# A one-layer hybrid decoder on one core: differential-attention weights split into two float32r halves, conv halos copied from PSUM, and one joint values product

## The chip, the core and the metric

The kernel runs on one core of one Trainium2 chip. The metric is the device time of one execution in microseconds (us); lower is better. Several executions were timed, and one more was recorded by the hardware profiler. The core has a matrix engine (TensorE, PE in the profile, with weight loads shown apart as PEld), three elementwise engines (VectorE = DVE, ScalarE = ACT, GpSimd = POOL), and a queue (SyncE = SP) that issues the DMAs here.

## The reference, cut to what the change touches

One layer maps 2048 tokens of width 1024 through three token mixers (a gated delta net, GDN; a dilated window attention; a differential attention), an output product, a LayerNorm, and a gated feed-forward block (FFN) with a short causal convolution. In the differential attention each of four heads has two softmax maps over the same values, and the second is subtracted with a weight:

```python
s = jnp.einsum('bhmqd,bhmkd->bhmqk', q_blk, k).astype(f32) * scale
s = jnp.where(kpos[None, :] <= qpos[:, None], s, -jnp.inf)
p = jax.nn.softmax(s, axis=-1)
return jnp.einsum('bhqk,bhkd->bhqd', p[:, :, 0] - lam * p[:, :, 1], v)
```

Both the GDN input and the FFN pass through a depthwise causal convolution over tokens:

```python
for j in range(1, K):
    y = y + xp[:, j:j + T] * w[j]
```

with K = 4 for the GDN and K = 3 for the FFN. The values of the dilated and of the differential attention are 256 columns each of one input product `x @ w_in`.

## The kernel before, in words

Tokens are cut into four blocks of 512 (`TB`). A product in full precision is made of three float32r products: each operand is split into a high half `hi` (a float32r cast) and a low half `lo` (the rest), and hi·hi, hi·lo and lo·hi are added in PSUM (lines 172 to 179). `weights` (lines 118 to 132) prepares the halves of a weight tile: one 512 KB DMA to `wraw`, a cast on ScalarE to `whi` (L130), a subtraction on GpSimd to `wlo` (L131). Such a tile serves 24 matmuls of 512 columns in a plain product.

Jobs are named by a letter and a token block: `A` projects for both attentions (`Projection.project`), `G` projects for the GDN with its convolution (`GatedInput.project`), `d` is the differential attention (`Diff.block`), `w` the dilated one, `i`, `b`, `p`, `r` are the stages of the GDN (invert, merge, prepare, recur), `o`, `t` and `f` are the output product, a transposition and the FFN block. Three lists, `FIRST`, `SECOND` and `THIRD` (lines 1331 to 1333), give the order in which the program is written; a scheduler of the framework then sets the order of the instructions on every engine by its own estimate of the times, and so mixes jobs. The GDN jobs are in `SECOND`, and the second list's PSUM pools are opened where the first list's are closed. Each engine carries out its own instructions in order.

**Values.** `Projection.values` (line 609) runs twice a block: once for the dilated attention (kind 0), whose stationary operand takes every fourth token, `v[k][:, n::4]`, and once for the differential one (kind 1), with 128 tokens side by side. The moving operand is 256 columns wide; a kind takes 96 matmuls and 2 weight tiles for a block.

**Weighted.** `Diff.weighted` (line 774) makes, for each pair of heads `i`, block `b` and 128 keys `kt`, and for each head `hh` of the pair, one step: two score matmuls (L796), two exponentials on ScalarE to `pd` and `pe` (L798), `pd = pd + nlam * pe` on VectorE (L802), and in the diagonal block a causal mask on GpSimd (L806). Two steps later (`LAG_PD`) a plain float32 matmul (L781) multiplies `pd` with 64 columns of values into half of the bank `po`. There are 160 steps: 16 in `d0`, 32, 48 and 64 in `d1` to `d3`.

**Halo.** A convolution copies a finished product from PSUM to `ub` behind the last 2 or 3 columns of the block before, kept in `halo` (GDN lines 328 to 330, 48 times; FFN lines 1052 to 1054, 172 times). Then one multiplication (L332, L1056) and two or three multiply-adds (L335, L1058) run on VectorE.

## Time and profile before

| what | value |
|---|---|
| median of 3 runs | 3292.51 us (3289.01 to 3293.84) |
| the profiled execution | 3297.27 us, its span 3295.6 us |
| mean granted TensorE clock | 0.967 |
| ScalarE busy | 1466.8 us (45%) |
| GpSimd busy | 1163.7 us (35%) |
| DMA moved | 434.19 MB, mean 132 GB/s |

The span runs from the first to the last instruction of the profiled execution. Busy times of TensorE add up instructions that overlap in its pipeline, so the cost of one matmul is read from the distance between two starts, not from its duration.

### The profile page before, as it was taken

To read this page: it belongs to the slowest core of one execution; us is meant where nothing else is said; L and a number is where in the kernel's file an instruction comes from. 1 tells how busy PE (TensorE), PEld (TensorE's weight loads), DVE (VectorE), ACT (ScalarE), POOL (GpSimd) and SP (SyncE) were. 2 spreads that over 40 slices of the span, in tenths; PEclk is the share of its full clock that TensorE was granted. 3 is DMA by queue.
4 is the path that set the end of the run, shared out by engine and by line. 5 is a ranking of instruction groups with operands and counts; after the bars stand their busy time and mean duration, and the time that the engine had idled before them with its cause. 6 is when DMAs were issued, how large, how long until landed. Compare 5 with 4: busy or idle time off the path is not lost. (4 is left out here: it accounts for less than half of the span.)

```text
span 3295.6 us, 42011 instructions
## 1 busy us (share of the span) xinstructions
PE 3073.1 (93%) x14860; PEld 2381.1 (72%) x14860; DVE 2328.9 (71%) x3958; ACT 1466.8 (45%) x2790; POOL 1163.7 (35%) x617
## 2 busy tenths in 40 slices
PE   7999987898898999999989999999999999999998
PEld 6768876676786787767866677777777664777776
DVE  3572689869557458777898667768988654787667
ACT  3543352343435335544755443344566445333223
POOL 3452443333225223334333332223333331344443
PEclk8999988998999999999999999999999998999999
DMA  6436373453756734333534334363533332432322
GB/s 201 147 132 191 105 215 110 132 155 104 216 169 185 232 108 138 104 97 115 169 99 147 98 106 133 99 201 102 181 104 108 96 93 74 132 121 90 96 85 82
DMA packets 286994, 434.19 MB, mean 132 GB/s; under 512 B 54624, under 2 KB 174944, under 8 KB 286016
## 3 DMA queue, kind: packets, MB, share of 16 engines
q1 hardware_dynamic: 286784, 431.51, 42.6%
q8 instruction: 117, 1.92, 0.2%
q14 instruction: 93, 0.76, 0.1%
HBM read 365.03 MB, written 66.26 MB: 131 GB/s over the span
## 5 line engine op out<-in xcount | busy, mean ns | idle before, releaser
L131 POOL TENSOR_TENSOR wlo<-wraw,whi 128x1024 fp32r<-128x1024 f32 x412 | 1011.2, 2456 | 1753.2 <-ACT whi L130 1577.1
L176 PE MATMUL d<-xhi,whi 128*128 128x512 f32 x2144 | 859.4, 401 | 27.1 <-ACT xhi L137 7.9
L178 PE MATMUL d<-xhi,wlo 128*128 128x512 f32 x2144 | 860.6, 402 | 15.3 <-POOL wlo L131 15.2
L177 PE MATMUL d<-xlo,whi 128*128 128x512 f32 x2144 | 856.6, 400 | 5.5 <-DVE xlo L139 5.5
L130 ACT CAST whi<-wraw 128x1024 fp32r<-128x1024 f32 x412 | 430.0, 1045 | 435.0 <-issue 160.0
L176 PEld LDWEIGHTS d<-xhi,whi 128*128 128x128 f32 x2144 | 411.4, 192 | 129.2 <-ACT whi L130 14.8
L178 PEld LDWEIGHTS d<-xhi,wlo 128*128 128x128 f32 x2144 | 411.1, 192 | 128.3 <-POOL wlo L131 23.0
L177 PEld LDWEIGHTS d<-xlo,whi 128*128 128x128 f32 x2144 | 411.2, 192 | 104.5 <-issue 13.8
L1054 DVE COPY c_halo<-ub 128x2 f32<-128x2 f32 x172 | 208.8, 1214 | 120.2 <-ACT ub L1053 119.6
L1121 PE MATMUL rp<-whi,hhi 128*128 128x512 f32 x704 | 268.8, 407 | 21.1 <-DVE r L1131 7.6
L1122 PE MATMUL rp<-wlo,hhi 128*128 128x512 f32 x704 | 282.2, 403 | 3.1 <-POOL wlo L131 2.9
L1124 PE MATMUL rp<-whi,hlo 128*128 128x512 f32 x672 | 269.8, 403 | 0.4 <-DVE hlo L1083 0.4
L739 ACT ACTIVATE bank<-bank,nm 128x512 f32<-128x512 f32 (+3 forms) x320 | 191.0, 597 | 130.5 <-DVE nm L735 72.9
L802 DVE SCALAR_TENSOR_TENSOR pd<-pe,f_nlam,pd 128x512 f32<-128x512 f32 (+3 forms) x160 | 138.0, 870 | 94.6 <-ACT pe L798 83.9
L735 DVE TENSOR_REDUCE nm<-bank 128x1 f32<-128x512 f32 (+3 forms) x288 | 163.3, 593 | 46.4 <-PE bank L730 45.9
L1121 PEld LDWEIGHTS rp<-whi,hhi 128*128 128x128 f32 x704 | 135.2, 193 | 61.5 <-issue 17.1
L1075 ACT ACTIVATE yg<-yg 128x512 f32<-128x512 f32 x88 | 55.5, 631 | 261.9 <-DVE yv L1074 250.7
L1058 DVE SCALAR_TENSOR_TENSOR yg<-ub,c_taps,yg 128x512 f32<-128x512 f32 x176 | 169.6, 963 | 2.4
L1122 PEld LDWEIGHTS rp<-wlo,hhi 128*128 128x128 f32 x704 | 135.6, 193 | 40.3 <-issue 6.8
L1124 PEld LDWEIGHTS rp<-whi,hlo 128*128 128x128 f32 x672 | 129.3, 193 | 34.6 <-issue 6.3
L1131 DVE TENSOR_TENSOR r<-r,rp 128x512 f32<-128x512 f32 x152 | 100.6, 681 | 69.6 <-PE rp L1124 61.2
L781 PE MATMUL bank<-pd,fv 128*64 128x512 f32 (+3 forms) x320 | 145.2, 563 | 4.3 <-DVE pd L802 2.2
(280 smaller groups left out, 5023.7 us busy)
## 6 DMA issues: line engine op xcount, KB each, us to landing
wraw<-in_w_up SPq DMA_DIRECT2D x172, 512.0 KB
wraw<-in_w_down SPq DMA_DIRECT2D x84, 512.0 KB
wraw<-in_w_gdn SPq DMA_DIRECT2D x64, 512.0 KB
ks<-fk_d SPq DMA_DIRECT2D x160, 196.0 KB
wraw<-in_w_out SPq DMA_DIRECT2D x40, 512.0 KB
wraw<-in_w_att SPq DMA_DIRECT2D x32, 512.0 KB
yraw<-y_d SPq DMA_DIRECT2D x48, 256.0 KB
xraw<-in_xT SPq DMA_DIRECT2D x40, 256.0 KB
```

The costliest lines, as they stand in the source:

```text
L130: nc.scalar.copy(hi, raw)
L131: nc.gpsimd.tensor_tensor(out=lo, in0=raw, in1=hi, op=ALU.subtract)
L176: nc.tensor.matmul(out=ps, lhsT=whi[:, k], rhs=xhi[k], start=(k == 0), stop=False)
L177: nc.tensor.matmul(out=ps, lhsT=whi[:, k], rhs=xlo[k], start=False, stop=False)
L178: nc.tensor.matmul(out=ps, lhsT=wlo[:, k], rhs=xhi[k], start=False, stop=(k == KD - 1))
L735: nc.vector.tensor_reduce(out=o, in_=s[:, 0:nf], axis=mybir.AxisListType.X, op=ALU.min)
L739: nc.scalar.activation(out=s[:, 0:n], in_=s[:, 0:n], func=AF.Exp, scale=-1.0, bias=o, accum_out=den[:, b, m, qt : qt + 1])
L1054: nc.vector.tensor_copy(self.halo[:, mt], ub[:, TB : TB + 2])
L1058: nc.vector.scalar_tensor_tensor(out=yc, in0=ub[:, j : j + TB], scalar=self.taps[:, mt, j : j + 1], in1=yc, op0=ALU.mult, op1=ALU.add)
L1121: nc.tensor.matmul(out=ps, lhsT=hi[:, sl], rhs=whi, start=first, stop=False)
L1122: nc.tensor.matmul(out=ps, lhsT=hi[:, sl], rhs=wlo, start=False, stop=last and lo is None)
L1124: nc.tensor.matmul(out=ps, lhsT=lo[:, sl], rhs=whi, start=False, stop=last)
```

## The change

Four things are changed.

1. The differential weights: `pe` now takes the sum, then ScalarE casts it to float32r (`ph`) and GpSimd subtracts that to get the rest (`pl`). The values are stored as 128 columns for each head, 64 high and 64 low, side by side. Two float32r matmuls (`ph`, then `pl`) past these 128 columns give the two halves of the result in the two halves of `po`'s partitions, and they are added at the end, once per head. One head is done after the other: `weighted` is called per head, `po` belongs to one head at a time. The product is three steps behind (`LAG_PD = 3`), `pd` has 2 buffers instead of 6, as `pe` has.
2. Each load of keys takes 2 maps of 256 keys instead of 4 of 128, and each load of values 2 x 128 columns; the number of loads is the same.
3. The convolutions: ScalarE copies the halo into `ub`, and VectorE saves the next halo from PSUM instead of from `ub`.
4. The values of both attentions are one product with 512 moving columns: 96 matmuls of 512 columns for a block instead of 192 of 256 (384 instead of 768 in all), 8 weight loads instead of 4 for a block, each serving 12 matmuls; the stationary operand is 128 tokens side by side for both. Two PSUM tiles are filled at a time.

```diff
-                nc.vector.tensor_copy(ub[:, 0:3], self.halo[:, mt])
+                nc.scalar.copy(ub[:, 0:3], self.halo[:, mt])
                 nc.scalar.copy(ub[:, 3:], pp)
-                nc.vector.tensor_copy(self.halo[:, mt], ub[:, TB : TB + 3])
+                nc.vector.tensor_copy(self.halo[:, mt], pp[:, TB - 3 : TB])
...
-        ws = [dn.weights(self.I["w_val"][kind, j], k=4, m=256) for j in range(2)]
         for g in range(2):
...
+            ps = [dn.ps.tile([P, TB], F32, tag="d", name="vp") for _ in range(2)]
+            for j in range(KD // 2):
+                whi, wlo = dn.weights(self.I["w_val"][j], k=2, m=TB)
+                for a in range(2):
+                    k = 2 * j + a
+                    for i in range(2):
+                        sl = slice((2 * g + i) * P, (2 * g + i + 1) * P)
+                        xhi, xlo = (v[k][:, sl] for v in x)
+                        nc.tensor.matmul(out=ps[i], lhsT=xhi, rhs=whi[:, a], start=(k == 0), stop=False)
+                        nc.tensor.matmul(out=ps[i], lhsT=xhi, rhs=wlo[:, a], start=False, stop=False)
+                        nc.tensor.matmul(out=ps[i], lhsT=xlo, rhs=whi[:, a], start=False, stop=(k == KD - 1))
+            for i in range(2):
...
+                nc.scalar.copy(vo, ps[i][:, 0:256])
+                nc.sync.dma_start(out=wide[n * P : (n + 1) * P].rearrange("t i c -> t (i c)"), in_=vo)
...
+                nc.scalar.copy(vs[:, :, 0], src)
+                nc.vector.tensor_tensor(out=vs[:, :, 1], in0=src, in1=vs[:, :, 0], op=ALU.subtract)
...
-            for hh in range(2):
-                nc.tensor.matmul(out=po[64 * hh : 64 * hh + 64, q0:], lhsT=v[:, 64 * hh : 64 * hh + 64],
-                                 rhs=pd[hh][:, q0:], start=start, stop=stop)
+            for part in (0, 1):
+                nc.tensor.matmul(out=po[:, q0:], lhsT=v, rhs=parts[part][:, q0:], start=start and part == 0, stop=stop and part == 1)
...
-                    pd = bp.tile([P, TB], F32, tag="pd", name="pd", bufs=NPD)
+                    pd = bp.tile([P, TB], F32, tag="pd", name="pd", bufs=NPE)
...
-                    nc.vector.scalar_tensor_tensor(out=pd[:, q0:], in0=pe[:, q0:], scalar=self.nlam, in1=pd[:, q0:],
+                    nc.vector.scalar_tensor_tensor(out=pe[:, q0:], in0=pe[:, q0:], scalar=self.nlam, in1=pd[:, q0:],
...
+                    ph = bp.tile([P, TB], F32R, tag="ph", name="ph", bufs=LAG_PD + 1)
+                    nc.scalar.copy(ph[:, q0:], pe[:, q0:])
+                    pl = bp.tile([P, TB], F32R, tag="pl", name="pl", bufs=LAG_PD + 1)
+                    nc.gpsimd.tensor_tensor(out=pl[:, q0:], in0=pe[:, q0:], in1=ph[:, q0:], op=ALU.subtract)
...
-            nc.vector.tensor_copy(ob, po)
+            o = ob[64 * hh : 64 * hh + 64]
+            nc.scalar.copy(o, po[64:P])
+            nc.vector.tensor_tensor(out=o, in0=po[0:64], in1=o, op=ALU.add)
...
-NPD = 6
...
-LAG_PD = 2
+LAG_PD = 3
```

The order of the instructions moves with it. On TensorE, where the GDN begins (`kk`, L420, is its first matmul), there stands before, in the middle of the convolution products `d` of job G1:

```order
L178 MATMUL d<-xhi,wlo 128x512
L420 MATMUL kk<-k 128x128
L176 MATMUL d<-xhi,whi 128x512
L177 MATMUL d<-xlo,whi 128x512
L420 MATMUL kk<-k 128x128 x3
```

and in the changed kernel, inside the values product `vp` of block 1:

```order
L624 MATMUL vp<-whi,xlo 128x512
L622 MATMUL vp<-whi,xhi 128x512 x2
L420 MATMUL kk<-k 128x128 x4
L623 MATMUL vp<-wlo,xhi 128x512
L624 MATMUL vp<-whi,xlo 128x512
```

Ahead of that first `kk` stood 1056 matmuls of products `d` and 384 of values; now 768 and 170 stand there, and 16 instead of 32 of the small product L304. From the first `kk` to the last GDN matmul (L565) stand 1344 `d` instead of 1056, 118 values instead of 192, and the same 182 of the output product; behind it 4320 `d` as before, 96 values instead of 192, and all the `weighted` products but those of `d0`.

On GpSimd, in the stage where `d2` runs among the FFN's products, only the mask stood between the halves of the weights before:

```order
L131 TENSOR_TENSOR wlo<-wraw,whi 128x1024 x9
L806 AFFINE_SELECT pd<-pd 128x128
L131 TENSOR_TENSOR wlo<-wraw,whi 128x1024
L806 AFFINE_SELECT pd<-pd 128x128 x3
L131 TENSOR_TENSOR wlo<-wraw,whi 128x1024
```

and now, at the start of `d2`, one or two subtractions `pl` stand ahead of each `wlo`:

```order
L819 TENSOR_TENSOR pl<-pe,ph 128x512
L131 TENSOR_TENSOR wlo<-wraw,whi 128x1024 x3
L819 TENSOR_TENSOR pl<-pe,ph 128x512 x2
L131 TENSOR_TENSOR wlo<-wraw,whi 128x1024
L819 TENSOR_TENSOR pl<-pe,ph 128x512 x2
```

On VectorE, in the FFN of the last block (`yg` and `yv` are the two convolutions, `hlo` the low half of the hidden tile), two small copies stood around each convolution before:

```order
L1052 COPY ub<-c_halo 128x2
L1054 COPY c_halo<-ub 128x2
L1056 TENSOR_SCALAR yv<-ub,c_taps 128x512
L1058 SCALAR_TENSOR_TENSOR yv<-ub,c_taps,yv 128x512 x2
L1074 TENSOR_TENSOR yv<-yv,yg 128x512
```

and now one, which reads the PSUM tile `d`:

```order
L1067 COPY c_halo<-d 128x2
L1069 TENSOR_SCALAR yv<-ub,c_taps 128x512
L1071 SCALAR_TENSOR_TENSOR yv<-ub,c_taps,yv 128x512 x2
L1087 TENSOR_TENSOR yv<-yv,yg 128x512
L1089 SCALAR_TENSOR_TENSOR yv<-yg,yv 128x512
```

The other small copy went to ScalarE's queue; the multiplication follows the remaining one as it did.

More of the change, by code (lines that the diff above doesn't have):

```diff
@@ L607, in product, with values @@
         return (yield from self.dn.product(w or self.dn.weights(self.I["w_att"][mt]), x))
-    def values(self, kind, x, dst):
+    def values(self, x, wide, near):
         nc, dn = self.nc, self.dn
-        ws = [dn.weights(self.I["w_val"][kind, j], k=4, m=256) for j in range(2)]
         for g in range(2):
-            ps = dn.ps.tile([P, 2, 256], F32, tag="d", name="vp")
-            for j in range(2):
-                n = 2 * g + j
-                for k in range(KD):
-                    whi, wlo = (w[:, k % 4] for w in ws[k // 4])
-                    xhi, xlo = (v[k][:, n::4] if kind == 0 else v[k][:, n * P : (n + 1) * P] for v in x)
-                    nc.tensor.matmul(out=ps[:, j], lhsT=xhi, rhs=whi, start=(k == 0), stop=False)
-                    nc.tensor.matmul(out=ps[:, j], lhsT=xhi, rhs=wlo, start=False, stop=False)
-                    nc.tensor.matmul(out=ps[:, j], lhsT=xlo, rhs=whi, start=False, stop=(k == KD - 1))
-                    yield SLOT
-            vo = self.ap.tile([P, 2, 2, 2, P], F32, tag="y", name="vo", bufs=NY)[:, 0]
-            nc.scalar.copy(vo, ps.rearrange("p j (i c) -> p i j c", i=2))
-            nc.sync.dma_start(out=dst[:, :, 2 * g : 2 * g + 2], in_=vo)
@@ new lines, in values @@
+            for i in range(2):
+                n = 2 * g + i
+                vo = self.ap.tile([P, 2, TB], F32, tag="y", name="vo", bufs=NY)[:, 0, 0:256]
+                nc.scalar.copy(vo, ps[i][:, 0:256])
+                nc.sync.dma_start(out=wide[n * P : (n + 1) * P].rearrange("t i c -> t (i c)"), in_=vo)
+                vs = self.ap.tile([P, 2, 4, 2, 64], F32R, tag="y", name="vs", bufs=NY)[:, 0]
+                src = ps[i][:, 256:].rearrange("p (h c) -> p h c", h=4)
+                nc.scalar.copy(vs[:, :, 0], src)
+                nc.vector.tensor_tensor(out=vs[:, :, 1], in0=src, in1=vs[:, :, 0], op=ALU.subtract)
+                nc.sync.dma_start(out=cast(near[:, :, n]), in_=cast(vs.rearrange("p h x c -> p h (x c)")))
@@ L662, in project @@
                     nc.sync.dma_start(out=cast(dst[32 * g : 32 * g + 32, mm]).rearrange("p m t -> m p t"), in_=parts[g])
-        for kind, dst in ((0, wv_d), (1, v_d)):
-            yield from self.values(kind, x, dst)
-        blocks[t] = (q_d, k_d, v_d, wq_d, wk_d, wl_d, wv_d)
+        yield from self.values(x, wv_d, v_d)
+        blocks[t] = (q_d, k_d, v_d, wq_d, wk_d, wl_d, wv_d.rearrange("(j r) i c -> j i r c", r=4))
 class Diff:
@@ L772, in stats, with weighted @@
         self.later.append([LAG_TURN, turn])
-    def weighted(self, t, i, qs):
+    def weighted(self, t, i, hh, qs, ob):
         nc, bp = self.nc, self.bp
@@ L795, in weighted @@
                         s = self.ps_s.get(False)
-                        nc.tensor.matmul(out=s[:, q0:], lhsT=ks[:, 2 * hh + m],
-                                         rhs=qs[:, 2 * hh + m, q0:], start=True, stop=True)
+                        nc.tensor.matmul(out=s[:, q0:], lhsT=ks[:, m, j * P : (j + 1) * P], rhs=qs[:, 2 * hh + m, q0:], start=True, stop=True)
                         nc.scalar.activation(out=e[:, q0:], in_=s[:, q0:], func=AF.Exp, scale=-1.0)
@@ L844, in block @@
             for i in range(2):
-                yield from self.weighted(t, i, qs[i])
+                ob = self.bp.tile([P, TB], F32, tag="ob", name="ob", bufs=1)
+                for hh in range(2):
+                    yield from self.weighted(t, i, hh, qs[i], ob)
             while self.later:
@@ L1051, in conv @@
         ub = hp.tile([P, TB + 2], F32, tag="ub", name="ub", bufs=NUB)
-        nc.vector.tensor_copy(ub[:, 0:2], self.halo[:, mt])
+        nc.scalar.copy(ub[:, 0:2], self.halo[:, mt])
         nc.scalar.copy(ub[:, 2:], pp)
-        nc.vector.tensor_copy(self.halo[:, mt], ub[:, TB : TB + 2])
+        nc.vector.tensor_copy(self.halo[:, mt], pp[:, TB - 2 : TB])
         yc = hp.tile([P, TB], F32, tag=tag, name=tag, bufs=NYG)
```

44 lines of the change are left out of this document (21 added, 23 removed).

## The prediction, made before the changed kernel was run

> **What bounds the kernel now.** The page comes first: busy time of each engine, then the slices.
>
> ```profile
> PE 3073.1 (93%) x14860; PEld 2381.1 (72%) x14860; DVE 2328.9 (71%) x3958; ACT 1466.8 (45%) x2790; POOL 1163.7 (35%) x617
> PE   7999987898898999999989999999999999999998
> DVE  3572689869557458777898667768988654787667
> ```
>
> TensorE is busy nearly everywhere, and VectorE is the only other engine that comes near, in the slices from the sixth to the tenth hundred us. Which stage that is, the first and last starts of two GDN lines tell (the query by source line):
>
> ```profile
> L420 PE MATMUL kk<-k x128: 270/275/582, 428.6 to 867.1; 128*128 128x128 f32 x128
> L567 DVE SCALAR_TENSOR_TENSOR yo<-yp,g_nwh,z x16: 734/748/752, 646.6 to 1071.1; 128x512 f32<-128x512 f32 x16
> ```
>
> So the GDN fills 428 to 1072 us. I cut the span there and around the end of `d3`; the columns are window, length, busy time of PE, PEld, DVE, ACT, POOL, granted clock and DMA.
>
> ```profile
> 0.00:428.00 428.00, 390.60 (x1849) 317.93 (x1850) 223.29 (x425) 180.25 (x332) 171.46 (x111) 0.96 0.50 157
> 428.00:1072.00 644.00, 551.97 (x3542) 462.50 (x3540) 480.94 (x862) 276.19 (x625) 237.34 (x158) 0.92 0.53 160
> 1072.00:2700.00 1628.00, 1579.49 (x7236) 1184.93 (x7237) 1215.88 (x2157) 797.09 (x1524) 536.97 (x251) 0.99 0.41 127
> 2700.00:2780.00 80.00, 72.76 (x206) 29.84 (x204) 40.59 (x56) 43.94 (x82) 13.11 (x17) 0.94 0.24 72
> 2780.00:3296.00 516.00, 478.30 (x2033) 385.91 (x2032) 368.18 (x460) 169.36 (x229) 204.82 (x82) 0.97 0.32 101
> ```
>
> From 1072 us on TensorE misses 49 of 1628 us: there a matmul saved is time saved. In the GDN it stands for 92 of 644 us at the least, the granted clock falls to 0.92, and VectorE is busy 75% of it in short dependent steps. There added matmuls can hide and saved ones can be lost. The 80 us up to 2780 are the end of `d3` with no other product beside it.
>
> **The matmuls, priced by their starts.** The timeline of TensorE shows a product, six starts apart five intervals:
>
> ```profile
> 1435.77 0.40 PE L177 MATMUL d<-xlo,whi 128*128 128x512 f32 x1
> ...
> 1436.91 0.39 PE L176 MATMUL d<-xhi,whi 128*128 128x512 f32 x1
> ```
>
> 1.14 us / 5 = 0.228 us for 512 float32r columns. The values product, kind 0 and then kind 1, ten intervals each:
>
> ```profile
> 80.07 0.40 PE L620 MATMUL vp<-whi,xhi 128*128 128x256 f32 x1
> ...
> 82.41 0.40 PE L621 MATMUL vp<-wlo,xhi 128*128 128x256 f32 x1
> 105.90 0.28 PE L620 MATMUL vp<-whi,xhi 128*128 128x256 f32 x1
> ...
> 107.10 0.28 PE L622 MATMUL vp<-whi,xlo 128*128 128x256 f32 x1
> ```
>
> 0.234 us with every fourth token as the stationary operand, 0.120 us with tokens side by side: the strided kind pays for 512 columns and gets 256. Before: 384 x 0.234 + 384 x 0.120 = 136 us. After: 384 x 0.228 = 88 us. **The joint product saves 48 us**, nearly all of it from the kind that was strided.
>
> The weighted product, one float32 matmul in two records:
>
> ```profile
> L781 PE MATMUL bank<-pd,fv 128*64 128x512 f32 x224 | 119.1, 631 | 3.7 <-DVE pd L802 2.2 <-POOL pd L806 1.1 <-DVE ob L822 0.4
> 1393.64 1.07 PE L781 MATMUL bank<-pd,fv 128*64 128x512 f32 x2
> 1394.65 0.50 PE L1124 MATMUL rp<-whi,hlo 128*128 128x512 f32 x1
> ```
>
> 1.01 us from its start to the next one's. 224 records are 112 matmuls of 512 columns: 113 us. The other 48 are 16 each of 384, 256 and 128 columns; by columns 16 x 1.01 x 1.5 = 24 us. After, each is two float32r matmuls, 0.456 us: 112 x 0.456 + 16 x 0.456 x 1.5 = 62 us. **The halves save 75 us.** Together 123 us of TensorE go.
>
> **Where they go.** The order rows above place them, and move other work. Ahead of the first `kk`: 288 products less (66 us), values 68 us before and 170 x 0.228 = 39 us now (29 less), `d0`'s weighted products 5 less, 16 of L304 4 less: 104 us off a stretch of 428. Inside the GDN: the 288 products and the 16 come in (+70), values fall from 34 to 27 us: +62. Behind it: values 12 less and the weighted products 70 less: 82 us. The sum is -104 + 62 - 82 = -124, as it must be.
>
> Ahead of the GDN I give back 5 us: a values weight tile now feeds 12 matmuls, 2.7 us, and must be loaded, cast and subtracted in that time.
>
> ```profile
> L131 POOL TENSOR_TENSOR wlo<-wraw,whi 128x1024 fp32r<-128x1024 f32 x412 | 1011.2, 2456 | 1753.2 <-ACT whi L130 1577.1 <-PE bank L730 30.8 <-PE bank L796 29.0
> L130 ACT CAST whi<-wraw 128x1024 fp32r<-128x1024 f32 x412 | 430.0, 1045 | 435.0 <-issue 160.0 <-PE rp L1124 104.8 <-PE d L177 90.8
> ```
>
> GpSimd's 2.46 us just fit; 16 more tiles (39 us GpSimd, 17 us ScalarE, 8 MB) have the scores and the dilated attention beside them, and if that cover fails each 8-tile group waits some microseconds. Bounds: 0 to 20 us. SP's queue gets the 16 loads and 16 more stores of values; key and value loads are as many as before, in longer rows. All of it falls under the same bound, with DMA at half its time or less in the windows above.
>
> Inside the GDN +62 us meets 92 idle ones, in pieces. I take half as hidden: +31, bounds 0 and +62.
>
> **The halo.** The copy out of `ub` is dear for two columns:
>
> ```profile
> L1054 DVE COPY c_halo<-ub 128x2 f32<-128x2 f32 x172 | 208.8, 1214 | 120.2 <-ACT ub L1053 119.6
> L1052 DVE COPY ub<-c_halo 128x2 f32<-128x2 f32 x172 | 48.7, 284 | 2.0
> L1056 DVE TENSOR_SCALAR yv<-ub,c_taps 128x512 f32<-128x512 f32 x84 | 43.3, 515 | 0.0
> L330 DVE COPY i_halo<-ub 128x3 f32<-128x3 f32 x28 | 28.8, 1027 | 19.4 <-ACT ub L329 18.5
> L332 DVE TENSOR_SCALAR yc<-ub,i_taps 128x512 f32<-128x512 f32 x28 | 19.2, 685 | 0.0
> L739 ACT ACTIVATION_READ_ACCUMULATOR bank<-bank,nm 128x1 f32 x320 | 64.3, 201 | 0.0
> ```
>
> It takes 1.2 us, its twin 0.28, and the multiplication right behind never waits. VectorE loses one copy and gets the other cheap (between 0.16 and 0.28 us; I take the lower), some 1.3 us for each convolution. ScalarE gets a copy of 2 columns, which no row shows; between 0.2 (one column) and 0.6 (512 columns, L798 below), near the first: 220 x 0.2 = 44 us on an engine 45% busy, hidden by its idle time. In the FFN VectorE is covered by the products, so nothing is gained there. In the GDN 28 convolutions, and nine or so moved in, are worth at most 28 x 1.0 = 28 us. The last two rows of VectorE are the GDN's own: there the multiplication takes 0.69 us and not 0.52, so whatever stretches the copy reaches the instruction behind it too. I take a third, 10 us.
>
> A rule gives a reason, and the sum stands without it. The Trainium skill, SBUF — State Buffer, section "Who interferes with whom", says that a copy or tensor_scalar of VectorE whose operands lie in SBUF can need the ports shared with GpSimd and then blocks until GpSimd's instruction ends, and one from PSUM does not. The 1.2 us beside GpSimd's 2.46 us agree. By that rule the halo copy from PSUM is free of the wait, but the multiplication behind it inherits what is left of it, and the GDN keeps most of the 28 us; without the rule it would gain them all. What is new in PSUM is that a product's bank is free only after VectorE has saved the halo: bounded by 0 and by 28 x 1.0 us the other way, taken as nothing since three banks of 24 matmuls (5.5 us each) rotate there.
>
> **The weighted steps.** Steps are counted by L802 in four windows, `d1`, `d2`, `d3` among products, and `d3` alone; then the engines' sum over them.
>
> ```profile
> 1372.00:1500.00 128.00, 25.95 (x29) 1.00 0.31 93
> 1700.00:1950.00 250.00, 46.06 (x48) 0.99 0.35 108
> 2560.00:2700.00 140.00, 23.06 (x28) 1.00 0.31 94
> 2700.00:2780.00 80.00, 25.85 (x36) 0.94 0.24 72
> sum 598.00, PE 584.44 PEld 368.44 DVE 391.93 ACT 289.29 POOL 186.90; mean PE 146.11 PEld 92.11 DVE 97.98 ACT 72.32 POOL 46.72
> ```
>
> Among products a step lasts 518 / 105 = 4.9 us, alone 80 / 36 = 2.2 us. What a step gains on the other engines:
>
> ```profile
> L798 ACT ACTIVATE pe<-bank 128x512 f32<-128x512 f32 x112 | 65.2, 597 | 77.5 <-PE bank L796 62.0 <-DVE pd L802 12.9 <-DVE r L1131 2.2
> L137 ACT CAST xhi<-xraw 128x512 fp32r<-128x512 f32 x40 | 24.4, 619 | 24.3 <-DMA xraw<-in_xT 23.5
> L346 POOL TENSOR_TENSOR isql<-isq,isqh 128x512 fp32r<-128x512 f32 x32 | 44.2, 1380 | 1.3
> L802 DVE SCALAR_TENSOR_TENSOR pd<-pe,f_nlam,pd x160: 339/746/2881, 135.0 to 2776.0; 128x512 f32<-128x512 f32 x112, 128x384 f32<-128x384 f32 x16, 128x256 f32<-128x256 f32 x16, 128x128 f32<-128x128 f32 x16
> ```
>
> ScalarE: two exponentials and a cast, 0.60 + 0.60 + 0.62 = 1.8 us a step. GpSimd: 1.38 us a step, for the 141 steps counted 195 us, at most 382 of 598 us busy. Neither becomes the bound among products. Alone, a step cannot be under ScalarE's 1.8 us, and `pe`, with two buffers, is held from its exponential to the end of `pl`: 0.60 + 0.75 + 0.62 + 1.38 = 3.4 us, 1.7 a step with no hand-off counted. The steps there take 2.2 us now over ScalarE's 1.2, so hand-offs cost up to 1.0, and I expect as much lost over the new 1.7 to 1.8 as makes 2.2 again: **the end of `d3` keeps its 80 us** and 36 x 0.55 = 20 us of the saving is lost there. For the in-order queues elsewhere (a `wlo` or a weight cast behind a `pl` or `ph` that waits, and the bank `po` handed from head to head 8 times more) I take 10 us; bounds 0 and 60.
>
> **Sum.** Ahead of the GDN -104 + 5; in it +31 - 10; behind it -82 + 20 + 10. That is -130. The profiled execution took 3297 us (span 3295.6 and 1.7 around it), so 3167; the median of the runs is 5 us lower, so **3162 us**.
>
> **Rivals.**
> - *The GDN grows by all that moves in.* Its PE idle time lies behind waits that the order keeps. +62, no halo gain, and the 20 us of weight supply: 3162 + 31 + 10 + 15 = 3218. For it: TensorE runs in order there. Against: VectorE, not TensorE, is what it waits for.
> - *The GDN hides everything.* 0 instead of +31, and VectorE's 28 us count in full: 3162 - 31 - 18 = 3113. For it: 75% VectorE.
> - *GpSimd holds VectorE.* L802's median is 0.75 us and its longest 2.9, so something blocks it at times. If each of 141 `pl` did so for its full 1.38 us, VectorE would have 392 + 195 = 587 us of work in windows that should shrink from 598 to 598 - 70 + 20 = 548: +39, 3201. It needs a two-input step of VectorE ready at every `pl`; I expect a third of it, which fits. The same page and section of the Trainium skill state that a VectorE instruction with two SBUF inputs contends with a GpSimd one that reads SBUF, a rule that speaks against this change; the spread of L802 agrees.
> - *Slower: the two `pe` buffers set the pace.* If, from exponential to the end of `pl`, queueing behind `wlo` (2.46 us) and VectorE's convolutions stretches 3.4 us to c, a step takes c / 2. Among products 105 steps then cost 105 x (c / 2 - 4.9) in place of the halves' gain. The rest of the change gives -104 + 5 + 21 - 12 = -90, so it turns slower from c / 2 = 5.8, c = 11.6 us; at c = 13, 3292 - 90 + 168 = 3370. For it: one `wlo` and one or two VectorE steps of 0.75 already make 7 us. Against: 11.6 needs two of each every time.
> - *The halves do not run at the product's pace.* Half the gain of 75 gone: 3200. Against: the score matmuls and products in the same stage are float32r of the same shape.
>
> **How the numbers follow.** Forecast 0.45 (3125 to 3195); GDN grows 0.15; GDN hides all 0.15; GpSimd holds VectorE 0.08; slow halves 0.04; buffers 0.10, of which 0.07 slower than before; a wash of these 0.03. The range takes the first five and their bounds, 3085 to 3245. A measurement of this kernel can tell about 0.2%, 7 us, from no change: faster 0.90, same 0.03, slower 0.07.
>
> **What would show it.** Values matmuls and the halves at starts 0.23 us apart; the first `kk` near 330 us and the GDN some 660 long; `c_halo` under 0.3 us with L1056's successor above 0.52; `d3` alone still near 80 us; GpSimd near 1390 us busy. Wrong would be: TensorE waiting for `pl` or for score banks among products (buffers), or a GDN of 700 us or more.

## The result, and the profile after

The changed kernel takes 3320.81 us (median of 4 runs, 3314.47 to 3322.21) against 3293.18 for the kernel before in the same session: a ratio of 1.0081, 95% interval 1.0069 to 1.0093. It is 0.8% slower; 3162 us and a gain were forecast. The profiled execution has a span of 3320.5 us against 3295.6. In the changed kernel the lines have moved; the names of the tiles have not.

The page of the changed kernel, busy time of each engine and the slices of TensorE and VectorE:

```profile
PE 2991.5 (90%) x14476; PEld 2356.1 (71%) x14476; DVE 2338.8 (70%) x3762; ACT 1593.8 (48%) x3216; POOL 1400.8 (42%) x793
PE   6789878888978899999998999999999988999998
DVE  2574397879646458777898767778998674786657
```

TensorE's busy time fell by 82 us, and yet the span grew by 25. GpSimd is at 1401 us (1390 was forecast). The same five stages as in the prediction, cut at the first `kk`, at the end of the GDN and around the end of `d3` (window, length, busy time of PE, PEld, DVE, ACT, POOL, granted clock, DMA):

```profile
0.00:357.00 357.00, 290.59 (x1312) 227.31 (x1312) 174.15 (x344) 167.24 (x330) 163.26 (x110) 0.92 0.55 173
357.00:1081.00 724.00, 620.95 (x3787) 511.26 (x3788) 519.12 (x906) 315.28 (x717) 294.76 (x187) 0.92 0.53 161
1081.00:2706.00 1625.00, 1527.32 (x7143) 1192.35 (x7144) 1244.09 (x2045) 872.21 (x1772) 683.05 (x363) 0.98 0.43 131
2706.00:2791.00 85.00, 70.00 (x203) 42.49 (x202) 48.66 (x54) 63.54 (x123) 55.82 (x54) 0.78 0.28 85
2791.00:3321.00 530.00, 482.68 (x2034) 382.64 (x2034) 352.83 (x414) 175.49 (x275) 203.93 (x83) 0.97 0.31 98
```

Against before: 428 to 357, 644 to 724, 1628 to 1625, 80 to 85, 516 to 530. The three stages behind the GDN were to shrink by 52 us and grew by 16. In the third, TensorE's idle time went from 49 to 98 us.

Where it went by kind of work, I summed over each trace the distances from every matmul's start to the next one's start, so a wait counts with the matmul ahead of it (us; `d` and `rp` are the products of the projections and the FFN, "scores" the matmuls of keys and queries in both passes):

```
                          d     rp  values  weighted  scores  rest    sum
before                 1673    740     148       140     172   408   3281
after                  1669    760     143       100     200   434   3306
expected of the change   0      0     -48       -75       0
measured                -4    +20      -5       -40     +28   +26    +25
```

So of 48 us in the values 5 are left, of 75 us in the weighted products 40, and the score matmuls, which nothing changed, lost 28. The waits of TensorE (the view of waits) in the third stage, before and then after, show on whom:

```profile
PE bank L730 <- ACT bank L739: 12.5, 25, 2.1
PE d L178 <- POOL wlo L131: 6.7, 7, 2.2
```

```profile
PE bank L791 <- ACT ph L817: 18.6, 18, 2.3
PE d L178 <- POOL wlo L131: 10.6, 12, 2.2
PE bank L805 <- ACT pd L806: 7.0, 7, 2.0
PE rp L1134 <- DVE r L1144: 6.8, 3, 2.9
PE rp L1134 <- DVE c_halo L1067: 6.0, 5, 1.9
...
PE bank L791 <- POOL pl L819: 3.4, 5, 1.7
```

The columns are us in total, times, and the longest. New are the waits for the halves of the weights, and for products' banks that VectorE holds until it has saved the halo. The combination of the two exponentials on VectorE in the kernel before, and then five groups of instructions of the changed kernel that belong to the change:

```profile
L802 DVE SCALAR_TENSOR_TENSOR pd<-pe,f_nlam,pd 128x512 f32<-128x512 f32 (+3 forms) x160 | 138.0, 870 | 94.6 <-ACT pe L798 83.9 <-ACT pd L798 10.5
```

```profile
L819 POOL TENSOR_TENSOR pl<-pe,ph 128x512 fp32r<-128x512 f32 (+3 forms) x160 | 197.9, 1246 | 116.2 <-ACT ph L817 113.2 <-PE d L177 2.7
L810 DVE SCALAR_TENSOR_TENSOR pe<-pe,f_nlam,pd 128x512 f32<-128x512 f32 (+3 forms) x160 | 163.3, 1025 | 98.5 <-ACT pe L806 93.7 <-ACT pd L806 3.2
L1067 DVE COPY c_halo<-d 128x2 f32<-128x2 f32 x172 | 26.7, 155 | 154.7 <-ACT ub L1066 154.2
L1069 DVE TENSOR_SCALAR yv<-ub,c_taps 128x512 f32<-128x512 f32 x84 | 152.3, 1814 | 0.0
L1065 ACT COPY ub<-c_halo 128x2 f32<-128x2 f32 x172 | 32.9, 192 | 395.1 <-DVE yg L1071 213.4 <-DVE yv L1071 174.2 <-DVE ds L764 3.6
```

The combination takes 1.03 us on average instead of 0.87. The halo copy fell from 1.21 to 0.16 us, and the multiplication `yv` behind it rose from 0.52 to 1.81. ScalarE's new copy of two columns lasts 0.19 us, but ScalarE stands still for 395 us ahead of it, waiting for VectorE to leave `ub`.

### The profile page after: what moved, and what is told of

The parts are those of the page before. It is cut to its first block, busy times and chain, and to the rows that moved or that the text cites. A ratio compares the mean times of both kernels' runs of the same rounds, so it can differ in the third digit from the quotient of the medians.

```text
span 3320.5 us, 41973 instructions
## 1 busy us (share of the span) xinstructions
PE 2991.5 (90%) x14476; PEld 2356.1 (71%) x14476; DVE 2338.8 (70%) x3762; ACT 1593.8 (48%) x3216; POOL 1400.8 (42%) x793
## 5 line engine op out<-in xcount | busy, mean ns | idle before, releaser
L131 POOL TENSOR_TENSOR wlo<-wraw,whi 128x1024 fp32r<-128x1024 f32 x428 | 1050.6, 2457 | 1540.5 <-ACT whi L130 1426.1
L130 ACT CAST whi<-wraw 128x1024 fp32r<-128x1024 f32 x428 | 446.5, 1045 | 338.1 <-issue 96.2
L819 POOL TENSOR_TENSOR pl<-pe,ph 128x512 fp32r<-128x512 f32 (+3 forms) x160 | 197.9, 1246 | 116.2 <-ACT ph L817 113.2
L810 DVE SCALAR_TENSOR_TENSOR pe<-pe,f_nlam,pd 128x512 f32<-128x512 f32 (+3 forms) x160 | 163.3, 1025 | 98.5 <-ACT pe L806 93.7
L1065 ACT COPY ub<-c_halo 128x2 f32<-128x2 f32 x172 | 32.9, 192 | 395.1 <-DVE yg L1071 213.4
L1069 DVE TENSOR_SCALAR yv<-ub,c_taps 128x512 f32<-128x512 f32 x84 | 152.3, 1814 | 0.0
L1071 DVE SCALAR_TENSOR_TENSOR yg<-ub,c_taps,yg 128x512 f32<-128x512 f32 x176 | 148.4, 843 | 2.6
L738 PE MATMUL bank<-ks,qs 96*128 96x512 f32 (+3 forms) x320 | 107.7, 383 | 43.1 <-DMA ks<-fk_d 33.9
```

Of the source, the lines that this page charges most:

```text
L130: nc.scalar.copy(hi, raw)
L131: nc.gpsimd.tensor_tensor(out=lo, in0=raw, in1=hi, op=ALU.subtract)
L810: nc.vector.scalar_tensor_tensor(out=pe[:, q0:], in0=pe[:, q0:], scalar=self.nlam, in1=pd[:, q0:], op0=ALU.mult, op1=ALU.add)
L819: nc.gpsimd.tensor_tensor(out=pl[:, q0:], in0=pe[:, q0:], in1=ph[:, q0:], op=ALU.subtract)
```

## The experiments

Each kernel's order on the engines is set anew by the scheduler's estimates, so two kernels differ in more than their edit. Six kernels with GpSimd's subtraction and the joint values took 3321 to 3334 us, so 13 us between two totals can be order alone. Where a smaller difference is used below, the length of a stage or a wait has to bear it out. In e6, e10, e11, e14 and e15 the high half is multiplied twice, and e12 and e16 have no low half: the low halves of the weights are missing from the results of these seven. The kernel before took 3293 to 3295 us beside all these runs.

| run | edit | median us | ratio to before, 95% interval |
|---|---|---|---|
| e1 | halo alone | 3312.20 | 1.0050 [1.0032, 1.0069] |
| e2 | joint values alone | 3281.31 | 0.9970 [0.9953, 0.9986] |
| e3 | halves alone | 3362.19 | 1.0203 [1.0184, 1.0222] |
| e4 | halves and joint values | 3328.11 | 1.0105 [1.0087, 1.0123] |
| e5 | change, halves made a step later | 3333.30 | 1.0112 [1.0095, 1.0130] |
| e6 | change without the subtraction | 3243.44 | 0.9849 [0.9828, 0.9871] |
| e7 | change, three `pe` buffers | 3333.45 | 1.0124 [1.0103, 1.0145] |
| e8 | change, old halo in the FFN | 3334.21 | 1.0119 [1.0101, 1.0137] |
| e9 | change, subtraction on VectorE | 3301.37 | 1.0022 [1.0009, 1.0035] |
| e10 | change, subtraction made but not used | 3327.71 | 1.0095 [1.0075, 1.0114] |
| e11 | e4 without the subtraction | 3266.42 | 0.9898 [0.9871, 0.9925] |
| e12 | e11, one float32r product, no cast | 3234.02 | 0.9808 [0.9791, 0.9824] |
| e13 | before, both values kinds side by side | 3284.09 | 0.9975 [0.9963, 0.9986] |
| e14 | e11 and a subtraction of 16 columns | 3270.18 | 0.9933 [0.9918, 0.9948] |
| e15 | e11 and a memset in its place | 3312.26 | 1.0060 [1.0041, 1.0078] |
| e16 | e12 with e13's values | 3219.87 | 0.9774 [0.9756, 0.9792] |
| e17 | before, FFN fill on ScalarE | 3325.65 | 1.0088 [1.0072, 1.0105] |
| e18 | before, FFN save from PSUM | 3285.65 | 0.9963 [0.9949, 0.9978] |

### The parts one by one: e1 to e4

```diff
# e1: the kernel before with the change's four halo lines
-        nc.vector.tensor_copy(ub[:, 0:2], self.halo[:, mt])
+        nc.scalar.copy(ub[:, 0:2], self.halo[:, mt])
-        nc.vector.tensor_copy(self.halo[:, mt], ub[:, TB : TB + 2])
+        nc.vector.tensor_copy(self.halo[:, mt], pp[:, TB - 2 : TB])
# e2: the kernel before with the change's product
-        for kind, dst in ((0, wv_d), (1, v_d)):
-            yield from self.values(kind, x, dst)
+        yield from self.values(x, wv_d, v_d)
# e3: the kernel before with the change's weighted() and the old values product, which stores high and low halves
# e4: the changed kernel with the four halo lines as before
```

> Only the halo copies of before are changed (ScalarE fills the halo into ub, VectorE saves the next one from PSUM). Theory 1 (the halo edit is the loss: the multiplication behind the copy inherits the wait for GpSimd, and ScalarE's early copy, which waits for VectorE to free ub, holds the weight casts behind it): 30 to 90 us slower than before, 3320 to 3385. Theory 2 (the weighted chain ph, pl is the loss): within 10 us of before. Theory 3 (the joint values product, by its weight loads and its place in the order, is the loss): within 10 us of before.

> Only the joint values product, with the values left in float32 and the weighted products as before. By the starts of the matmuls it saves 48 us of TensorE. Theory 1 and theory 2: 20 to 48 us faster than before, 3245 to 3275. Theory 3: no gain or slower, 3290 to 3330.

> Only the differential weights in two float32r halves, one head after the other, product three steps behind; values as two products and the halo as before. By the starts it saves 75 us of TensorE, 20 of them lost at the end of d3. Theory 1 and theory 3: 30 to 60 us faster than before, 3230 to 3265. Theory 2: no gain or slower, 3290 to 3340.

> The changed kernel with the halo copies as before: halves and joint values together. Theory 1: 60 to 120 us faster than the changed kernel, 3200 to 3260. Theory 2 or theory 3: within 20 us of the changed kernel, 3300 to 3340.

The halves alone cost 67 us, where they take 75 us of work off TensorE; the halo alone costs 17; the values alone gain 14 of 48. All three were gains in the prediction. e1 and e2 fell between the ranges expected of them, e3 beyond both. The three add up to 70 us and the whole change costs 28, so the parts aren't independent: with the joint values beside them the halves cost 47 (e2 to e4). The start distances of e3 against before: weighted 140 to 108, scores 172 to 202, and 43 more in the rest. So the halves are the main loss, by what they do to the work around them.

### What in the halves costs: e5, e6, e7, e9, e10

```diff
# e5: one step later, with four `pe` buffers
-                    ph = bp.tile(...); nc.scalar.copy(ph, pe); pl = ...
+                    wait.append((q0, pe, vs[:, j], ...))
+                    if len(wait) > 1:
+                        halves(*wait.pop(0))
# e6: no pl
-                    nc.gpsimd.tensor_tensor(out=pl[:, q0:], in0=pe[:, q0:], in1=ph[:, q0:], op=ALU.subtract)
-                    put.append((q0, (ph, pl), vs[:, j], ...))
+                    put.append((q0, (ph, ph), vs[:, j], ...))
# e7 (three small tiles of the statistics get one buffer instead of two)
-                    pe = bp.tile([P, TB], F32, tag="pe", name="pe", bufs=NPE)
+                    pe = bp.tile([P, TB], F32, tag="pe", name="pe", bufs=NPE + 1)
# e9
-                    nc.gpsimd.tensor_tensor(out=pl[:, q0:], in0=pe[:, q0:], in1=ph[:, q0:], op=ALU.subtract)
+                    nc.vector.tensor_tensor(out=pl[:, q0:], in0=pe[:, q0:], in1=ph[:, q0:], op=ALU.subtract)
# e10: pl is made as in the change
-                    put.append((q0, (ph, pl), vs[:, j], ...))
+                    put.append((q0, (ph, ph), vs[:, j], ...))
```

> The changed kernel, but the two halves of a step are made one step later (after the exponentials of the next step), with four `pe` buffers and three of `ph` and `pl`; the product stays three steps behind. Theory A (in-order wait: the cast to `ph` stands in ScalarE's queue waiting for VectorE's combination, and the next step's exponentials stand behind it): the rows that name ph as what PE waits for go, and the time falls by 30 to 60 us, to 3260-3290. Theory B (GpSimd's subtraction is what comes too late): the low half now has one step less, time 3320 +-10. Theory C (two `pe` buffers pace): falls by about the same as in e7.

> The changed kernel without GpSimd's subtraction: the low half isn't made, and the high half is multiplied twice, so TensorE's work is the same and the output lacks the low halves. Theory B (GpSimd's subtraction is the loss, 198 us of GpSimd and its wait): 3260-3290. Theory A (ScalarE's cast waiting in order is the loss): 3305-3320, and waits for ph remain. Theory C: `pe` is freed one operation sooner, 3300-3315.

> The changed kernel with three `pe` buffers instead of two (three small one-use tiles of the softmax statistics get one buffer instead of two to make room). Theory C (an exponential waits for a `pe` that the halves still read): 3270-3300. Theories A and B: 3310-3322, within 0.3% of the changed kernel.

> The changed kernel with the low half subtracted on VectorE instead of GpSimd (160 operations of some 0.75 us, 120 us more of VectorE; GpSimd back to about 1200 us). Theory B1 (GpSimd is the loss: its in-order queue and the time it takes from VectorE): 3250-3290. Theory B2 (one more link between the exponential and the product is the loss, whoever carries it): 3310-3340. Theory D (only the order that the scheduler writes differs between such kernels): 3310-3330, as all those with a low half.

> The changed kernel where GpSimd still makes the low half, but no matmul reads it: the high half is multiplied twice, so TensorE's and GpSimd's work are as in the changed kernel, the low halves are left out of the result, and TensorE waits for GpSimd's subtraction nowhere. B1 (load and queue of GpSimd): 3300-3325, as the changed kernel. B2 (the link that TensorE waits for): 3240-3260, as without the subtraction.

Neither the later step nor the third buffer helps (both runs end a little above every range expected of them): ScalarE's wait in order and the two `pe` buffers, as I had them, are not the loss. Without the subtraction 77 us go. They stay gone in no kernel that still carries it out on GpSimd: in e10 no matmul reads the low half, TensorE waits for `pl` nowhere, and the time is 3328. So the loss isn't one more link between exponential and product; it is the 198 us of GpSimd's work.

Some 20 of the 77 us are the luck of e6's order: no subtraction stands in the GDN, and from the first `kk` to the last GDN row it takes 704 us in e6, but 718 to 730 in the changed kernel, e4, e5, e7 to e11, e14 and e15. Behind the GDN, where 144 of the 160 subtractions stand, the profiled executions take 2239 us with the subtraction and 2183 without: 56 us. That is the price; 38 us of it are more idle time of TensorE.

On VectorE the subtraction costs 58 us over e6 (3301), 39 of them behind the GDN, less than on GpSimd, though VectorE was the busier engine by far; e9 fell between its two ranges. VectorE's combination in e6, e9 and e10:

```profile
L810 DVE SCALAR_TENSOR_TENSOR pe<-pe,f_nlam,pd 128x512 f32<-128x512 f32 (+3 forms) x160 | 135.3, 856 | 61.1 <-ACT pe L806 44.9 <-ACT pd L806 15.6
```

```profile
L810 DVE SCALAR_TENSOR_TENSOR pe<-pe,f_nlam,pd 128x512 f32<-128x512 f32 (+3 forms) x160 | 126.0, 800 | 30.8 <-ACT pe L806 27.8 <-ACT pd L806 2.4
```

```profile
L810 DVE SCALAR_TENSOR_TENSOR pe<-pe,f_nlam,pd 128x512 f32<-128x512 f32 (+3 forms) x160 | 156.0, 979 | 90.4 <-ACT pe L806 78.1 <-ACT pd L806 4.5 <-POOL pl L819 2.5
```

0.86, 0.80 and 0.98 us: where GpSimd subtracts, VectorE's operation beside it is longer. The seven kernels of this study in which GpSimd subtracts whole tiles of weights show 0.91 to 1.05 us, the others 0.80 to 0.89, but for e12 with 0.92.

### How GpSimd's work costs: e11, e14, e15

```diff
# e11: e4 with e6's edit; e14 and e15 add one instruction to e11
# e14
+                    pl = bp.tile([P, 16], F32R, tag="pl", name="pl", bufs=LAG_PD + 1)
+                    nc.gpsimd.tensor_tensor(out=pl, in0=pe[:, TB - 16 :], in1=ph[:, TB - 16 :], op=ALU.subtract)
# e15
-                    pe = bp.tile([P, TB], F32, tag="pe", name="pe", bufs=NPE)
+                    full = bp.tile([P, 1280], F32, tag="pe", name="pe", bufs=NPE)
+                    pe = full[:, 0:TB]
...
+                    nc.gpsimd.memset(full, 0.0)
```

> The halves and the joint values with the old halo (3328 us), without the subtraction: the high half is multiplied twice, the low halves are left out. If the 77 us that went with the subtraction are its price and not the luck of one order: 3245-3265. If it was the order: 3290-3330.

> As e11 (3266 us; high half multiplied twice, low halves left out of the result), with a subtraction of only 16 columns on GpSimd in every step, behind the cast: GpSimd waits in its queue for the cast as in the changed kernel, but works next to nothing there. If the wait in the in-order queue is the price (weights' low halves stand behind it): 3310-3330. If the work is: 3260-3275.

> As e11, with a memset of 128 x 1280 on GpSimd in every step in the subtraction's place (it overwrites the spent pe tile behind the cast, so it waits for the same cast, holds the same tile and lasts about as long), low halves left out of the result. It writes and reads nothing. If the price is what GpSimd's reads take from two-input operations of VectorE: 3265-3295, with VectorE's combination near 0.89 us as in e11. If the price is GpSimd's time itself (queue, tile held, exclusive port): 3310-3335.

With the old halo the subtraction is worth 62 us (e4 to e11), and 62 behind the GDN as well (2244 and 2183 us). So its price holds in two quite different orders. The short subtraction, which waits in the same queue for the same cast, costs 4 us, which is within the noise; GpSimd's in-order wait is not the price. The memset reads nothing and lasts nearly as long (186.6 us in all; 196.9 for the subtraction in e4). It costs 46 us by the medians, and 34 behind the GDN in the profiled execution. VectorE's combination and its copy of the halo into `ub` in e11, e4 and e15 (the groups of instructions):

```profile
L810 DVE SCALAR_TENSOR_TENSOR pe<-pe,f_nlam,pd 128x512 f32<-128x512 f32 (+3 forms) x160 | 141.3, 891 | 77.7 <-ACT pe L806 64.3 <-ACT pd L806 10.3 <-POOL wlo L131 2.9
...
L1063 DVE COPY ub<-c_halo 128x2 f32<-128x2 f32 x172 | 45.5, 265 | 2.6 <-DMA y_d<-yo 0.7
```

```profile
L810 DVE SCALAR_TENSOR_TENSOR pe<-pe,f_nlam,pd 128x512 f32<-128x512 f32 (+3 forms) x160 | 147.7, 926 | 76.5 <-ACT pe L806 65.8 <-ACT pd L806 6.8 <-POOL pl L819 1.9
...
L1065 DVE COPY ub<-c_halo 128x2 f32<-128x2 f32 x172 | 61.4, 357 | 2.2 <-DMA y_d<-yo 0.4
```

```profile
L811 DVE SCALAR_TENSOR_TENSOR pe<-pe,f_nlam,pd 128x512 f32<-128x512 f32 (+3 forms) x160 | 136.5, 856 | 74.0 <-ACT pe L807 70.5 <-ACT pd L807 2.7 <-issue 0.3
...
L1065 DVE COPY ub<-c_halo 128x2 f32<-128x2 f32 x172 | 64.1, 373 | 3.1 <-DMA y_d<-yo 1.2
```

By their pages VectorE is busy 2331 us without, 2417 with the subtraction, 2372 with the memset. The averages above mix two kinds of instruction, which the timelines tell apart. A halo copy beside a `wlo` in the kernel before, a combination beside the subtraction in e4, and one beside the memset in e15:

```profile
1246.84 2.39 POOL L131 TENSOR_TENSOR wlo<-wraw,whi 128x1024 fp32r<-128x1024 f32 x1 [2.41 <-ACT whi L130]
1247.28 1.98 DVE L1054 COPY c_halo<-ub 128x2 f32<-128x2 f32 x1 [0.66 <-ACT ub L1053]
```

```profile
1919.79 1.29 POOL L819 TENSOR_TENSOR pl<-pe,ph 128x512 fp32r<-128x512 f32 x1 [2.73 <-ACT ph L817]
1920.24 1.39 DVE L810 SCALAR_TENSOR_TENSOR pe<-pe,f_nlam,pd 128x512 f32<-128x512 f32 x1 [0.50 <-ACT pe L806]
```

```profile
1815.72 1.17 POOL L819 MEMSET pe<- 128x1280 f32 x1 [3.84 <-ACT ph L818]
1816.19 0.75 DVE L811 SCALAR_TENSOR_TENSOR pe<-pe,f_nlam,pd 128x512 f32<-128x512 f32 x1 [1.11 <-ACT pe L807]
```

The copy ends 0.03 us after GpSimd's instruction and the first combination 0.55 us after it; the second combination takes no notice of the memset. It is so throughout. In the kernel before, the 61 halo copies out of `ub` that start while GpSimd stands idle take 0.16 us, and the 106 that start inside a `wlo` take 1.87 us on average and all end 0.02 to 0.03 us after it. In e4 a combination of 512 columns takes 0.745 us beside an idle GpSimd; the 20 that start inside a subtraction take 1.18 us on average and all end 0.55 us after it. In e15 the 27 that start inside a memset take 0.75 us, but the 10 fills of `ub` that start inside one all end only after it. So where the two contend, VectorE's instruction is held until GpSimd's has ended.

That is what the Trainium skill, SBUF — State Buffer, section "Who interferes with whom", states: an operation of VectorE with two inputs in SBUF contends with a GpSimd instruction that reads SBUF and not with one that only writes it, while a copy in a two-port mode contends with GpSimd, and the later one waits for the whole instruction. The traces agree, by the numbers above.

They also show how much is held. I compared each VectorE instruction that starts inside GpSimd's with the median of the same ones beside an idle GpSimd; the sums are estimates from these durations. The subtraction holds VectorE for 45 us in the changed kernel and 54 in e4, the memset for 32 in e15; the prices behind the GDN are 56, 62 and 34. The price follows the held time, and VectorE's idle time did not absorb it. That nothing else carries a part of it isn't shown: the memset also holds `pe` longer and moves the order. Nor is it settled what the reads alone cost. I had expected the memset to cost either little or the whole; more than half of the price comes with an instruction that only writes, and the other 16 us by the medians (28 behind the GDN) are too near to the 13 that the order can make.

### The values: e13

```diff
-                    xhi, xlo = (v[k][:, n::4] if kind == 0 else v[k][:, n * P : (n + 1) * P] for v in x)
+                    xhi, xlo = (v[k][:, n * P : (n + 1) * P] for v in x)
```

and the dilated values are stored by tokens, as in the change.

> The kernel before, with one edit: the dilated values take 128 tokens side by side as the stationary operand as the other kind does; both keep 256 columns, the old weight tiles (4 a block, each for 48 matmuls) and the old order of the code. TensorE saves 384 x (0.234 - 0.120) = 44 us of the joint product's 48. If the joint product lost its gain to weight supply: 3255-3270, below the 3281 of the joint values alone. If the GDN stage absorbs what moves into it: 3278-3290.

TensorE saves 41 us of busy time (3073.1 to 3031.9), and the run 9 us. The weight tiles are the old ones, so the supply of weights isn't what ate the gain of the joint product, which is as small. TensorE's waits up to 140 us in before, e13 and after show one piece of where it went:

```profile
PE bank L730 <- DMA ks<-fk_d: 13.7, 1, 13.7
```

```profile
PE bank L737 <- DMA ks<-fk_d: 22.2, 2, 12.6
```

```profile
PE bank L738 <- DMA ks<-fk_d: 31.2, 2, 18.8
```

The values product stood beside the round trip of block 0's keys through memory. With the product made shorter, TensorE waits for those keys instead: 8.5 us more in e13, 17.5 in the changed kernel and in e2 alike.

### The halo: e8, e17, e18

```diff
# e8: the changed kernel with the FFN's two lines as before
# e17: the kernel before
-        nc.vector.tensor_copy(ub[:, 0:2], self.halo[:, mt])
+        nc.scalar.copy(ub[:, 0:2], self.halo[:, mt])
# e18: the kernel before
-        nc.vector.tensor_copy(self.halo[:, mt], ub[:, TB : TB + 2])
+        nc.vector.tensor_copy(self.halo[:, mt], pp[:, TB - 2 : TB])
```

> The changed kernel with the halo lines of the FFN as they were before (those of the GDN stay changed). If the halo edit costs 13 us in the last, FFN-only stage and does nothing else: 3305-3310, with that stage back at 516 us. If the slot of VectorE that it frees was a help in the mixed stages: above 3310.

> The kernel before with one line changed: the FFN's fill of ub with the halo runs on ScalarE; the halo is saved from ub as before. Theory F (ScalarE stands at the fill, which waits for VectorE to leave ub, and the casts of weights wait behind it): the FFN-only stage grows from 516 to 526-534 us, ScalarE's fill is the line with idle time. Theory G (PSUM save): the stage stays at 514-518.

> The kernel before with one line changed: the FFN's halo is saved from PSUM; the fill stays on VectorE. Theory G: the FFN-only stage 526-534 us, with the multiplication at 1.6 to 1.8 us. Theory F: the multiplication at 1.6 to 1.8 us too, but the stage at 508-518, and the whole at or below the kernel before.

The edit's halves have opposite signs. From the last combination of `d3` to the end of the span is the FFN-only stage: 520 us before, 534 in the changed kernel, 535 in e1, 538 in e17 (at most 534 was expected), 510 in e18. The order hardly moves this stage: it takes 518 to 522 us in all eleven kernels with both old halo lines in the FFN and 532 to 538 in all seven with both new ones. ScalarE's copies to `ub` in before, and its new one in e17:

```profile
L1053 ACT COPY ub<-d 128x512 f32<-128x512 f32 x172 | 99.8, 580 | 27.6 <-DVE yg L1058 17.0 <-DVE yv L1058 5.9 <-PE d L178 4.5
```

```profile
L1052 ACT COPY ub<-c_halo 128x2 f32<-128x2 f32 x172 | 33.0, 192 | 424.3 <-DVE yg L1058 225.9 <-DVE yv L1058 194.4 <-DMA y_d<-yo 3.3
```

The fill needs no product, only a free `ub`. So it stands early in ScalarE's queue, and ScalarE waits 424 us there for VectorE, with the casts of weights behind it in order; with the fill on VectorE ScalarE waited 28 us for the same tile. What comes late then is seen at TensorE, in the FFN-only stage from 2800 to 3290 us, before and in e1, where the fill is on ScalarE too:

```profile
L178 PE MATMUL d<-xhi,wlo 128*128 128x512 f32 x384 | 150.6, 393 | 3.2 <-POOL wlo L131 3.1
...
L1122 PE MATMUL rp<-wlo,hhi 128*128 128x512 f32 x224 | 89.9, 404 | 2.1 <-POOL wlo L131 1.9
```

```profile
L178 PE MATMUL d<-xhi,wlo 128*128 128x512 f32 x384 | 151.7, 396 | 9.1 <-POOL wlo L131 9.1
...
L1122 PE MATMUL rp<-wlo,hhi 128*128 128x512 f32 x205 | 83.5, 411 | 5.5 <-POOL wlo L131 5.5
```

The waits for the low halves of weights, which GpSimd makes from ScalarE's casts, go from 5 to 15 us, and to 17 in e17. The save from PSUM gains 10 us alone, and this stage is 9 us shorter by it, though the multiplication inherits most of the wait (1.35 us here, under the 1.6 to 1.8 expected):

```profile
L1054 DVE COPY c_halo<-d 128x2 f32<-128x2 f32 x172 | 26.3, 153 | 122.7 <-ACT ub L1053 122.2
...
L1056 DVE TENSOR_SCALAR yv<-ub,c_taps 128x512 f32<-128x512 f32 x84 | 113.0, 1345 | 0.0
```

e8 is not settled: its FFN-only stage is back at 520 us, 14 less, and yet the kernel is 13 us slower than the changed one. In the profiled executions it loses 21 us in the stages before, by VectorE's fuller queue there or by the scheduler's other order; no run tells these apart.

### Versions that beat both: e12 and e16

```diff
# e12, on e11
-                    nc.vector.scalar_tensor_tensor(out=pe[:, q0:], ...)
+                    nc.vector.scalar_tensor_tensor(out=ph[:, q0:], ...)
-                    nc.scalar.copy(ph[:, q0:], pe[:, q0:])
...
-            for part in (0, 1):
-                nc.tensor.matmul(out=po[:, q0:], lhsT=v, rhs=parts[part][:, q0:], ...)
+            nc.tensor.matmul(out=po[:, q0:], lhsT=v, rhs=parts[0][:, q0:], ...)
# e16: the same, with e13's values product and the low half of the values stored beside the high one
```

> As e11, but VectorE writes the high half itself, the cast on ScalarE and the second matmul are gone: the weights are rounded to float32r and their low halves left out of the result. TensorE has 62 / 2 = 31 us less, ScalarE about 97 us less. If TensorE's work is what counts once the chain is as short as before: 3205-3235, below the kernel before. If the cast on ScalarE was no cost: 31 us below e11.

> e13's values with e12's weighted step (float32r weights written by VectorE, one matmul past 128 columns, low halves left out), old halo. The gains should add if they lie in different stages: 3234 less the difference of e13 to 3281, 3210-3225. If they compete for the same idle time: 3230-3240.

One product with weights rounded to float32r takes 3234 us, 32 less than e11. That is about the 31 us that the second matmul was worth, so by these totals ScalarE's cast, which also went, shows no gain of its own. With e13's values it takes 3220, 2.3% under the kernel before. e6, e11 and e14 are faster than the kernel before too, but like these two they leave out the low halves of the weights. Of the versions that leave nothing out, e2, e13 and e18 are each 9 to 14 us faster than before; they were not tried together.

## Why the prediction was wrong, point by point

- **The matmuls' prices held.** The timeline of TensorE shows the halves among the products at the pace forecast, 0.23 us to the next start:

```profile
1799.63 0.39 PE L791 MATMUL bank<-ph,fv 128*128 128x512 f32 x1
1799.86 0.40 PE L177 MATMUL d<-xlo,whi 128*128 128x512 f32 x1
...
1801.02 0.39 PE L791 MATMUL bank<-pl,fv 128*128 128x512 f32 x1
1801.25 0.39 PE L176 MATMUL d<-xhi,whi 128*128 128x512 f32 x1
```

- **Ahead of the GDN, -104 + 5: it became -71.** The first `kk` came at 357 us and not near 330. The step that failed is "Ahead of the GDN I give back 5 us": I looked for the price in the weights' supply and not in what the shortened product had covered. The keys' round trip accounts for 17.5 us of the 28. The joint values alone bring the first `kk` to 345 us (e2), so the other 12 us or so come with the rest of the change, and what costs them is open.
- **"Inside the GDN +62 us meets 92 idle ones, in pieces. I take half as hidden": nothing was hidden.** TensorE's busy time there grew by 69 us and its idle time from 92 to 103, so the stage grew by 80. The joint values alone show the same (e2), with `kk` at 344.9 and the last GDN row at 1061.0:

```profile
345.00:1062.00 717.00, 612.32 (x3754) 503.79 (x3755) 520.58 (x926) 304.45 (x672) 281.44 (x184) 0.92 0.52 158
```

  Busy time +60, length +73. The rival in which the GDN grows by all that moves in was right in this stage; it even grew by a little more. The halo's 10 us can't be seen in it.
- **"In the FFN VectorE is covered by the products, so nothing is gained there": 14 us were lost.** I priced ScalarE's copy by its 0.2 us and "hidden by its idle time", and not by where it stands in ScalarE's queue and what it waits for (e17). That the multiplication inherits the wait was forecast for the GDN, and it does so in both; by e18 that was harmless.
- **Behind the GDN, -82 + 20 + 10: it became +16.** `d3` alone took 85 us, near the expected 80. What failed is the term of 10 us, bounds 0 and 60, "for the in-order queues elsewhere", together with the rival in which GpSimd holds VectorE, of which I expected "a third of it, which fits". The subtraction costs 56 to 62 us behind the GDN (e6, e11), most of the halves' gain there. By e10 and e14 it does so neither through the link nor through the wait in GpSimd's queue, but through GpSimd's work itself. The prediction added up VectorE's and GpSimd's work and asked whether it fits the window. It did fit: VectorE was held for 45 us, less than a third of the rival's 195. But the held time went to the span nearly whole, and for that no term was there; even with all 195 us held the rival came to +39 only. Without the subtraction these stages shrink by 42 us (e6), near the forecast 52.
- **The two `pe` buffers** were the rival on the slower side. The kernel did get slower, but a third buffer didn't help (e7), nor four (e5): the sign was right, not the mechanism. Both signs of being wrong came, a GDN of 724 us and TensorE waiting for `ph` and `pl` among the products; by e10 the waits for `pl` are not the loss.

By stages: forecast -99, +21, -52; measured -71, +80, +16. The difference of 155 us is 28 ahead of the GDN, 59 in it, and 68 behind it.

## What to carry to other kernels

An elementwise operation moved to an engine that has time is not free when its instructions hold those of a busier engine: look in the trace at how long the neighbour's instructions take with and without it beside them, and put an unused copy of it into the kernel and time that before building on it. Work that a stage of short dependent steps absorbs only counts as hidden if the stage's idle time shrinks in a trace; here it did not, and a product that covers a round trip through memory gives little back when shortened. A small instruction with few dependencies goes early into an in-order queue, and whatever it waits for then holds all that stands behind it.

## What the runs showed of the hardware that was not expected

After the wait of 3.1 us at the first `kk` TensorE runs at about half its pace for some microseconds. The timeline of the changed kernel at the first `kk`:

```profile
357.23 1.44 PE L420 MATMUL kk<-k 128*128 128x128 f32 x8 [3.12 <-DMA k<-qk_d]
...
359.31 0.63 PE L623 MATMUL vp<-wlo,xhi 128*128 128x512 f32 x1
359.74 0.63 PE L624 MATMUL vp<-whi,xlo 128*128 128x512 f32 x1
...
361.62 0.40 PE L623 MATMUL vp<-wlo,xhi 128*128 128x512 f32 x1
361.85 0.40 PE L624 MATMUL vp<-whi,xlo 128*128 128x512 f32 x1
```

Starts are 0.43 us apart, then 0.23; from 359 to 361 us the granted clock is 0.50. The Trainium skill, TensorE: Matmul & The Clock Gate, section "Part 1: The HAM clock gate (the "warmup" mystery)", names two clocks with 0.427 us for 512 columns at the lower one, taken up after an idle window of about 3.4 us; the 0.43 us agree, and here a wait of 3.1 us was enough. So a wait can cost more than its length. In the window of `d3` alone the granted clock fell from 0.94 to 0.78, and over the whole run from 0.967 to 0.955: 1 - 0.955 of 3320 us is 149 us, against 109 before. A part of that falls into the waits themselves, where there is no matmul to slow.

A copy of two columns out of SBUF takes VectorE 0.16 us beside an idle GpSimd, as little as out of PSUM (0.15). The average of 1.2 us is the wait for a `wlo`, and moving the copy to PSUM hands that wait to the next operation that reads SBUF alone: in e18 the 60 multiplications beside an idle GpSimd take 0.47 us, and the 108 that start inside a `wlo` 2.04. By the same estimate as above, `wlo` holds VectorE for 518 us in the kernel before, out of 2329 us that its profile calls busy. So a good part of a busy share can be waiting.
